# Splitting attention weights: low parts by an accumulating transfer, q and k normalised on VectorE

## Chip, cores and metric

One of the cores of a Trainium2 chip runs the whole program: five engines (TensorE, written PE in the profile, with its weight loads as PEld; VectorE, DVE; ScalarE, ACT; GpSimd, POOL; SyncE, SP, which here only issues transfers) and 16 DMA engines. The metric is the device time of one execution in microseconds. Lower is better.

## What is computed

A causal decoder trunk of two layers over 512 tokens of width 1024, in float32. Each layer is an attention block and a squared-ReLU MLP, both behind an RMSNorm:

```python
def reference(x, ...):
    for layer in range(DEPTH):                       # 2
        h = rms_norm(x, g_mix[layer])
        x = x + (even_mixer if layer % 2 == 0 else odd_mixer)(h, ...)
        h = rms_norm(x, g_mlp[layer])
        x = x + squared_relu_mlp(h, w_up[layer], w_down[layer])
    return x

def odd_mixer(h, w_in, b_forget, c_q_gain, c_k_gain, w_out):
    proj = jnp.einsum("bsd,de->bse", h, w_in)
    q = rms_norm(proj[..., :w].reshape(bsz, seq, 16, 64), c_q_gain)
    k = rms_norm(proj[..., w:2 * w].reshape(bsz, seq, 16, 64), c_k_gain)
    ...
    y = forgetting_attention(q, k, v, log_f)
    return jnp.einsum("bse,ed->bsd", y, w_out)
```

The even mixer does the same with two kinds of heads (eight with dilated windows, "a"; eight with a window of 128 and sinks, "b"), the odd one with sixteen forgetting heads ("c"). q and k are normalised per head.

## The kernel before

**Split products.** Every large product is made of three TensorE passes over numbers of the type fp32r. A weight W is split into a high part `whi` (W copied, and so rounded, to fp32r) and a low part `wlo` = W - `whi`; the activations are split likewise, and a product is x_hi·whi + x_hi·wlo + x_lo·whi (lines 230 to 232 in the projections, 163, 166 and 167 in `mm3` elsewhere).

**Weights of the attention.** `load_w` (line 177) fetches a tile `wraw` of 128 x 1024 numbers by SP and cuts it into parts of 128 x 512, which `parts` (line 169) hands to `split` (line 146). An entry of a pattern says who does what: the first word is the engine of `whi` (`act`: a ScalarE copy, line 149; `pool`: a GpSimd multiplication by 1.0, line 151), the second that of the subtraction for `wlo` (line 154, VectorE or GpSimd). `PAT_ATT` is for the projections, `PAT_OP` for the output projection, `PAT_START` (`act`, `dve`) for the first projections of each layer and for `kv_b`; a counter goes through a pattern part by part. There are four `wraw` buffers (the tiles `xl` of the residual use them too) and seven each of `whi` and `wlo`. With 8 parts for 512 columns, 4 for 256, 8 for the 272 of `vf_c` and 16 for an output projection, the two attention layers have 52 and 68 parts: 64 go by `PAT_ATT`, 32 by `PAT_OP`, 24 by `PAT_START`, of which 4 are those of `kv_b`. The MLP splits its weights elsewhere (`halves`, lines 768 and 769).

**Normalisation.** `norm_heads` (line 239) copies a projection's four token tiles out of PSUM, squares and sums them by head, takes reciprocal roots (`rsqrt_small`, lines 128 to 133) and multiplies (line 259). `NORM = 'vgvg'` gives the multiplications of tiles 0 and 2 to VectorE and of 1 and 3 to GpSimd. Eight calls make 32 multiplications, 28 of them 512 wide.

**Heads.** `prep_q` and `prep_k` transpose q and k by TensorE and split them (lines 276, 277, 158, 159); the halves of K are swapped by a transfer from SBUF to SBUF on SP (line 289). `scores` makes a head's scores, the maxima (VectorE, line 338), the exponentials (ScalarE, 341) and multiplies by the reciprocal sums: GpSimd does three of the four tiles (line 349), ScalarE one (346). `values` transposes these (361), splits them (373 and 374) and multiplies by v (381).

**Order.** `run` (line 429) interleaves the generators of the heads with those of the next projection or of the output projection, and `out_part` (line 461) is the dense work at the end of each attention; the MLP follows. Beyond that the library arranges each engine's instructions when the program is built, by its own estimates of when their inputs are ready; only what is marked `keep_in_program_order` keeps its place. On the chip each engine takes its instructions in that fixed order, and so does each engine's queue of transfers: a transfer that waits holds those behind it.

Of the kernel before, what the change touches and what calls it, by code (L numbers as in the profile page):

```python
# [9 lines left out]
F32 = mybir.dt.float32  # L10
# [3 lines left out]
AF = mybir.ActivationFunctionType  # L14
OP = mybir.AluOpType
# [14 lines left out]
RAW = 4  # L30
NHI = 7
NLO = 7
PAT_OP = (('pool', 'pool'), ('pool', 'dve'), ('pool', 'dve'), ('act', 'pool'))
SQ = (4, 4, 5, 5, 6, 6, 7, 7, 10)
R = 6
PAT_START = (('act', 'dve'), ('act', 'dve'))
WARM = 24
NORM = 'vgvg'
PSC = 'ggga'
GRAIN = 4  # L40
STARTPIN = 4
# [22 lines left out]
LAGS = (1, 1, 1)  # L64
NB = 86
PAT_MLP = (("act", "dve"),)
PAT_ATT = (('pool', 'dve'), ('pool', 'pool'))
YLO = 'dve'
SSQ = "vector"

# [1 line left out]
def trunk(ctx, tc, x, g_mix, g_mlp, w_in_even, a_q_gain, a_k_gain, b_q_gain, b_k_gain, b_sinks,  # L72
          w_out_even, w_in_odd, b_forget, c_q_gain, c_k_gain, w_out_odd, w_up, w_down, out):
    nc = tc.nc
# [4 lines left out]
    act = ctx.enter_context(tc.tile_pool(name="act", bufs=14))  # L79
# [4 lines left out]
    def bank(tag, name):  # L84
        return ps.tile([P, 512], F32, tag=tag, bufs=BANKS[tag], name=name)
# [56 lines left out]
    def in_order(m):  # L142
        if cnt["start"]:
            tc.keep_in_program_order(m)

    def split(dst_h, dst_l, src, eng, lo="dve"):

        if eng == "act":
            in_order(nc.scalar.copy(dst_h, src))  # L149
        elif eng == "pool":  # L150
            nc.gpsimd.tensor_scalar(dst_h, src, 1.0, 1.0, op0=OP.mult, op1=OP.mult)  # L151
        else:
            nc.vector.tensor_copy(dst_h, src)
        in_order((nc.gpsimd if lo == "pool" else nc.vector).tensor_sub(dst_l, src, dst_h.bitcast(F32)))  # L154
# [14 lines left out]
    def parts(src, eng):  # L169

        shape = list(src.shape)
        hi = wp.tile(shape, F32R, tag="whi", bufs=NHI, name="whi")
        lo = wp.tile(shape, F32R, tag="wlo", bufs=NLO, name="wlo")
        split(hi, lo, src, *eng)
        return hi, lo

    def load_w(srcs, w, kw, pat):
# [13 lines left out]
    def layer_attention(li, hT, w_in, w_out, stats=None):  # L191


        with ExitStack() as c2:
# [10 lines left out]

            def project(cols, use, pat=PAT_ATT, ahead=False):

                n = sum(b - a for a, b in cols)
                outs = [bank("pA", f"pj{t}") for t in range(NT)]
                pairs = 0  # L210
                kw = 4 if n == 256 else 2
                w = 1024 // kw if n <= 512 and n in (256, 512) else n
                for k0 in range(0, DC, kw):
                    srcs, o = [], 0
                    for a, b in cols:
                        srcs.append((0, o, w_in[k0 * P:(k0 + kw) * P, a:b]))
                        o += b - a
                    ws = load_w(srcs, w, kw, pat)
                    if ahead:
                        yield 0  # L220

                    last = k0 + kw == DC
                    for m in range(NT if last else kw):
                        for k, t in ([(k0 + kk, m) for kk in range(kw)] if last else [(k0 + m, t) for t in range(NT)]):
                            kk = k - k0
                            o = outs[t][:, :n]
                            ts = slice(t * P, (t + 1) * P)
                            xh, xl = hT[k][:, 0, ts], hT[k][:, 1, ts]
                            hi, lo = ws[kk]
                            nc.tensor.matmul(o, xh, hi[:, :n], start=k == 0, stop=False)  # L230
                            nc.tensor.matmul(o, xh, lo[:, :n], start=False, stop=False)  # L231
                            nc.tensor.matmul(o, xl, hi[:, :n], start=False, stop=k == DC - 1)  # L232
                            pairs += 1
                            if pairs % GRAIN == 0:
                                yield GRAIN / 32 * n
                use(outs)
                yield 0

            def norm_heads(outs, nh, sq_tag="sq", sq_bufs=1 + li):
# [16 lines left out]
                for t in range(NT):  # L256
                    q = qk[t // 2][:, t % 2, :w].rearrange("p (h d) -> p h d", d=HD)
                    eng = nc.gpsimd if NORM[t] == "g" else nc.vector
                    eng.tensor_mul(q, q, rs[:, t, :nh].unsqueeze(2).to_broadcast([P, nh, HD]))
# [188 lines left out]
            def out_weights(pairs, c0):  # L448
# [4 lines left out]
                while k < np_:  # L453
# [4 lines left out]
                    k = m + 1  # L458
                return load_w(runs, w, np_, PAT_OP)

# [47 lines left out]
            if li == 0:  # L508
                def qk_a(g):
                    return project([(g * 256, g * 256 + 256), (512 + g * 256, 512 + g * 256 + 256)], qk_use(g, 8),  # L510
                                   *((PAT_START, True) if g == 0 else ()))

                def v_a(g):
                    return project([(1024 + g * 256, 1024 + g * 256 + 256)], v_use(g, 0), PAT_START if g == 0 else PAT_ATT)

                def att_a(g):
                    def get(p_):
                        qk = st["qk", g]
                        return prep_q(qk, p_ * P), prep_k(qk, 256 + p_ * P, gg[:, 0:1])
                    return attend(get, 256, lambda: st["v", g], lambda j: j, "a", 4 * g, 2, 2 * g)  # L520

                def kv_b():
                    def use(outs):
                        st["v", 3] = prep_v(outs, P, 2, 1)
                        st["k", "b"] = norm_heads(outs, 2)
                    return project([(2048, 2304)], use, PAT_START)

                def att_b():
                    def get(p_):
                        if p_ == 0:  # L530
                            st["kb"] = prep_k(st["k", "b"], 0, gg[:, 1:2])
                        k = st["kb"][p_ // 2]
                        return prep_q(st["qk", "b"], p_ * P), [k, k]
                    return attend(get, 0, lambda: st["v", 3], lambda j: j // 4, "b", 0, 4, 4)

                tables, first, qk0 = make_tables(ap, dist, lt, lb), start(ap, hT), qk_a(0)
                next(tables)
                for i, n in enumerate((1, 1 + 8 // GRAIN, 1 + 8 // GRAIN, 1 + 8 // GRAIN)):
                    cnt["start"] = i < STARTPIN
                    next(first)  # L540
                    for _ in range(n):
                        next(qk0)
                    if i == 0:
                        next(tables)
                cnt["start"] = False
                for _ in range(8 // GRAIN):
                    next(qk0)
                next(first)
                all_of(qk0)
                all_of(v_a(0))  # L550
                run(att_a(0), 32, chain(kv_b(), project([(1536, 2048)], qk_use("b", 8))), 768, LEADS[0])
                run(att_b(), NB, chain(qk_a(1), v_a(1)), 768, LEADS[1])
                run(chain(att_a(1), last_values()), 38, chain(out_part([0, 1, 4, 5], True),
                                                              out_part([6, 7], False), ahead([2, 3])), 1536, LEADS[2])
                last = [2, 3]
            else:
                def qk_c(g):
                    return project([(g * 256, g * 256 + 256), (1024 + g * 256, 1024 + g * 256 + 256)], qk_use(g, 8))

                def v_c(g):  # L560
                    return project([(2048 + g * 256, 2048 + g * 256 + 256)], v_use(g, g))

                def vf_c():
                    def use(outs):
                        forget(ap, outs)
                        v_use(0, 0)(outs)
                    return project([(2048, 2304), (3072, 3088)], use, PAT_START)

                def att_c(g):
                    def get(p_):  # L570
                        qk = st["qk", g]
                        return prep_q(qk, p_ * P), prep_k(qk, 256 + p_ * P, gg[:, 2:3])
                    return attend(get, 256, lambda: st["v", g], lambda j: j, "c", 4 * g, 2, 2 * g)

                g = vf_c()
                for _ in range(STATS):
                    next(g)
                stats()
                all_of(g)
                all_of(qk_c(0))  # L580
                for g in range(3):
                    run(att_c(g), 36, chain(qk_c(g + 1), v_c(g + 1)), 768, LEADS[3 + g])
                run(chain(att_c(3), last_values()), 42, chain(out_part([0, 1, 2, 3], True),
                                                              out_part([4, 5], False), ahead([6, 7])), 1536, LEADS[6])
                last = [6, 7]
# [659 lines left out]
```

## Time and profile before

| | before |
|---|---|
| median of 3 runs | 1168.34 us (1167.92 to 1168.7) |
| profiled execution, its own time | 1168.43 us |
| its span | 1166.7 us |
| granted TensorE clock | 0.999 |
| attention of layer 0, about | 0 to 229 us |
| MLP of layer 0, about | 229 to 572 us |
| attention of layer 1, about | 572 to 829 us |
| MLP of layer 1, about | 829 us to the end |

The span is what the profile shows of one execution; 1.7 us of its time lie around it. The stages are read from the first instructions of each in the timeline; a stage's first weights are split before it begins. A busy TensorE isn't TensorE at its peak: matmuls overlap, each shown from its start to a modelled end.

### The profile page before, as it was taken

To read this page: it belongs to the slowest core of one execution; us is meant where nothing else is said; L and a number is where in the kernel's file an instruction comes from. 1 tells how busy PE (TensorE), PEld (TensorE's weight loads), DVE (VectorE), ACT (ScalarE), POOL (GpSimd) and SP (SyncE) were. 2 spreads that over 40 slices of the span, in tenths; PEclk is the share of its full clock that TensorE was granted. 3 is DMA by queue.
4 is the path that set the end of the run, shared out by engine and by line. 5 is a ranking of instruction groups with operands and counts; after the bars stand their busy time and mean duration, and the time that the engine had idled before them with its cause. 6 is when DMAs were issued, how large, how long until landed. Compare 5 with 4: busy or idle time off the path is not lost.

```text
span 1166.7 us, 17503 instructions
## 1 busy us (share of the span) xinstructions
PE 1146.8 (98%) x6256; PEld 982.5 (84%) x6256; DVE 880.7 (75%) x1877; ACT 647.1 (55%) x1349; POOL 202.4 (17%) x296
## 2 busy tenths in 40 slices
PE   8999989999999999999999999999999999999998
PEld 7987877888988988988887888888888888888887
DVE  7878999968858857855647877788858759669676
ACT  6555867556545545444235675656756455465452
POOL 1345444200000000000255445332100000000000
PEclk9999999999999999999999999999999999999999
DMA  7522014242333333333443333343430721623403
GB/s 253 163 76 89 19 57 146 70 126 78 104 108 91 91 108 91 106 111 110 146 128 109 107 84 109 107 118 113 163 105 4 235 87 55 198 73 109 147 33 109
DMA packets 100655, 126.57 MB, mean 108 GB/s; under 512 B 6184, under 2 KB 79944, under 8 KB 100568
## 3 DMA queue, kind: packets, MB, share of 16 engines
q1 hardware_dynamic: 99384, 121.23, 34.3%
q10 hardware_dynamic: 608, 2.13, 0.5%
q0 software_dynamic: 576, 2.10, 0.4%
q8 instruction: 49, 0.80, 0.3%
q14 instruction: 38, 0.31, 0.1%
HBM read 112.29 MB, written 6.32 MB: 102 GB/s over the span
## 4 chain that ended last, share of the span: by engine, by line
PE 85%; DVE 8%; DMA 2%; POOL 1%; issue 1%; ACT 1%; SPq 0%; ACTq 0%; POOLq 0%; DVEq 0%
PE up L163 10%; PE up L167 10%; PE up L166 10%; PE pj L230 5%; PE pj L232 5%; PE pj L231 5%; PE O L381 3%; PE PT L361 2%; PE Y L1021 2%; PE Y L1019 2%; PE Y L1022 2%; PE op L167 2%; PE op L163 2%; PE op L166 2%; PE Y L1068 1%; PE S L324 1%
## 5 line engine op out<-in xcount | busy, mean ns | idle before, releaser
L163 PE MATMUL up<-xin,whi 128*128 128x512 f32 x512 | 200.5, 392 | 0.0
L167 PE MATMUL up<-xin,whi 128*128 128x512 f32 x512 | 199.3, 389 | 0.0
L166 PE MATMUL up<-xin,wlo 128*128 128x512 f32 x512 | 199.2, 389 | 0.0
L768 ACT CAST whi<-wraw 128x512 fp32r<-128x512 f32 x228 | 139.2, 619 | 105.0 <-PE up L167 47.7
L769 DVE TENSOR_TENSOR wlo<-wraw,whi 128x512 fp32r<-128x512 f32 x228 | 151.7, 686 | 50.8 <-ACT whi L768 50.5
L167 PEld LDWEIGHTS up<-xin,whi 128*128 128x128 f32 x512 | 96.1, 188 | 20.1
L166 PEld LDWEIGHTS up<-xin,wlo 128*128 128x128 f32 x512 | 96.2, 188 | 19.8 <-issue 0.2
L163 PEld LDWEIGHTS up<-xin,whi 128*128 128x128 f32 x512 | 96.1, 188 | 19.8 <-issue 0.2
L341 ACT ACTIVATE P<-P,negm 128x128 f32<-128x128 f32 (+5 forms) x128 | 69.5, 544 | 51.7 <-DVE negm L338 47.9
L950 ACT ACTIVATE u<-up 128x512 f32<-128x512 f32 x64 | 38.3, 599 | 90.9 <-PE up L167 90.8
L230 PE MATMUL pj<-whi,hn 128*128 128x512 f32 (+2 forms) x256 | 88.7, 346 | 0.0
L232 PE MATMUL pj<-whi,hn 128*128 128x512 f32 (+2 forms) x256 | 86.9, 339 | 0.0
L231 PE MATMUL pj<-wlo,hn 128*128 128x512 f32 (+2 forms) x256 | 86.8, 339 | 0.0
L151 POOL TENSOR_SCALAR whi<-wraw 128x512 fp32r<-128x512 f32 x88 | 60.5, 689 | 143.0 <-PE pj L232 121.8
L789 DVE TENSOR_TENSOR t<-u 128x256 f32<-128x256 f32 x56 | 23.2, 424 | 62.8 <-ACT u L1093 61.0
L154 POOL TENSOR_TENSOR wlo<-wraw,whi 128x512 fp32r<-128x512 f32 x48 | 64.4, 1346 | 20.7 <-ACT whi L149 17.9
L230 PE MATMUL pj<-whi,h 128*128 128x512 f32 (+1 forms) x192 | 66.5, 353 | 0.7 <-DVE v L159 0.7
L232 PE MATMUL pj<-whi,h 128*128 128x512 f32 (+1 forms) x192 | 65.5, 343 | 0.0
L231 PE MATMUL pj<-wlo,h 128*128 128x512 f32 (+1 forms) x192 | 65.5, 341 | 0.0
L349 POOL TENSOR_SCALAR P<-P,rden 128x256 f32<-128x256 f32 (+2 forms) x96 | 47.7, 500 | 90.8 <-DVE rden L344 90.0
L154 DVE TENSOR_TENSOR wlo<-wraw,whi 128x512 fp32r<-128x512 f32 (+1 forms) x72 | 49.9, 700 | 17.7 <-POOL whi L151 14.5
L373 ACT CAST PT<-PT 128x256 fp32r<-128x256 f32 (+3 forms) x128 | 49.5, 405 | 19.4 <-PE PT L361 18.5
(229 smaller groups left out, 3054.4 us busy)
## 6 DMA issues: line engine op xcount, KB each, us to landing
wraw<-in_w_up SPq DMA_DIRECT2D x64, 512.0 KB, 3.8
wraw<-in_w_down SPq DMA_DIRECT2D x56, 512.0 KB, 4.2
wraw<-in_w_in_odd SPq DMA_DIRECT2D x36, 256.0 KB, 3.3
mraw<-in_w_down SPq DMA_DIRECT2D x16, 512.0 KB, 4.4
K<-K SPq DMA_DIRECT2D x26, 256.0 KB
wraw<-in_w_in_even SPq DMA_DIRECT2D x10, 512.0 KB, 4.0
wraw<-in_w_in_even SPq DMA_DIRECT2D x16, 256.0 KB, 4.5
xl<-xsp SPq DMA_DIRECT2D x8, 512.0 KB
```

The costliest lines, as they stand in the source:

```text
L151: nc.gpsimd.tensor_scalar(dst_h, src, 1.0, 1.0, op0=OP.mult, op1=OP.mult)
L154: in_order((nc.gpsimd if lo == "pool" else nc.vector).tensor_sub(dst_l, src, dst_h.bitcast(F32)))
L163: m = nc.tensor.matmul(o, wh, xh, start=start, stop=False, skip_group_check=more)
L166: nc.tensor.matmul(o, wl, xh, start=False, stop=False, skip_group_check=more)
L167: nc.tensor.matmul(o, wh, xl, start=False, stop=stop, skip_group_check=more)
L230: nc.tensor.matmul(o, xh, hi[:, :n], start=k == 0, stop=False)
L231: nc.tensor.matmul(o, xh, lo[:, :n], start=False, stop=False)
L232: nc.tensor.matmul(o, xl, hi[:, :n], start=False, stop=k == DC - 1)
L341: nc.scalar.activation(p[:, :ne], p[:, :ne], AF.Exp, scale=-1.0, bias=negm[:, i:i + 1], accum_out=den[:, i:i + 1])
L373: nc.scalar.copy(dst[:, 0], pt[:, :n])
L768: sca(nc.scalar.copy(dst_h, src))
L769: late.append(lambda: vec(nc.vector.tensor_sub(dst_l, src, dst_h.bitcast(F32))))
```

## The change

The 64 parts of `PAT_ATT`, the 32 of `PAT_OP` and the 4 of `kv_b`, which now takes `PAT_ATT`, get their low parts in another way. `lo` is first written with minus W, rounded to fp32r as `whi` is, by the one of GpSimd and ScalarE that does not make `whi`; then a transfer that GpSimd issues adds `wraw` onto it, which leaves W - `whi`. The two engines swap roles from part to part. No subtraction is left for these 100 parts; the 20 other parts of the attention are split as before. And all multiplications of `norm_heads` go to VectorE.

```diff
-PAT_OP = (('pool', 'pool'), ('pool', 'dve'), ('pool', 'dve'), ('act', 'pool'))
+PAT_OP = (('pool', 'dma'), ('act', 'dma'))
-NORM = 'vgvg'
+NORM = 'vvvv'
-PAT_ATT = (('pool', 'dve'), ('pool', 'pool'))
+PAT_ATT = (('pool', 'dma'), ('act', 'dma'))
...
         hi = wp.tile(shape, F32R, tag="whi", bufs=NHI, name="whi")
         lo = wp.tile(shape, F32R, tag="wlo", bufs=NLO, name="wlo")
-        split(hi, lo, src, *eng)
+        if eng[1] == "dma":
+
+            if eng[0] == "act":
+                nc.scalar.copy(hi, src)
+                nc.gpsimd.tensor_scalar(lo, src, -1.0, 1.0, op0=OP.mult, op1=OP.mult)
+            else:
+                nc.gpsimd.tensor_scalar(hi, src, 1.0, 1.0, op0=OP.mult, op1=OP.mult)
+                nc.scalar.activation(lo, src, AF.Copy, scale=-1.0)
+            nc.gpsimd.dma_start(lo.bitcast(F32), src, accum_op=OP.add)
+        else:
+            split(hi, lo, src, *eng)
         return hi, lo
...
-                    return project([(2048, 2304)], use, PAT_START)
+                    return project([(2048, 2304)], use)
```

## The prediction

> **What bounds the kernel now.** I read the page first, then the busy time of the engines by stretch, then what TensorE waited for in each stretch of the attention, then the chain of work through those waits.
>
> ```profile
> PE 1146.8 (98%) x6256; PEld 982.5 (84%) x6256; DVE 880.7 (75%) x1877; ACT 647.1 (55%) x1349; POOL 202.4 (17%) x296
> ```
>
> TensorE is busy for 98% of the span, and the change takes no matmul away; only the time in which TensorE waits can shrink. Where it lies:
>
> ```profile
> 25.00:225.00 200.00, 192.34 (x1145) 164.48 (x1144) 174.27 (x488) 129.78 (x336) 85.12 (x139) 1.00 0.32 96
> 225.00:575.00 350.00, 349.49 (x2025) 309.84 (x2024) 252.38 (x465) 180.85 (x327) 0.31 (x1) 1.00 0.34 103
> 600.00:825.00 225.00, 221.87 (x1327) 189.05 (x1326) 174.14 (x459) 136.34 (x322) 96.30 (x125) 1.00 0.38 108
> ```
>
> The columns are stretch, length, then busy time of PE, PEld, DVE, ACT, POOL, the granted clock, DMA share and GB/s. The middle row, an MLP, has TensorE idle for 0.5 us of 350. The two attention stretches have it idle for 200 - 192.3 = 7.7 and 225 - 221.9 = 3.1 us. That is a ceiling of about 11 us (0.9%) for anything done to the attention's other engines. A finer cut shows where VectorE is the cause:
>
> ```profile
> 125.00:150.00 25.00, 24.98 (x175) 21.93 (x174) 23.46 (x82) 22.08 (x67) 12.34 (x32) 1.00 0.08 23
> 150.00:175.00 25.00, 21.79 (x143) 19.13 (x141) 24.51 (x71) 15.18 (x42) 8.03 (x15) 1.00 0.22 66
> ```
>
> At 150 to 175 us VectorE is busy for 24.5 of 25 and TensorE for 21.8: there TensorE waits for VectorE. The waits of TensorE themselves, from the view of waits taken by stretch (the first two rows from 100 to 125 us, two from 150 to 175, one from 175 to 200, the last from 575 to 650; total, times, longest):
>
> ```profile
> PE qkT L266 <- DVE qk L259: 1.3, 2, 0.9
> PE S L324 <- DVE Q L277: 0.3, 1, 0.3
> ...
> PE S L324 <- DVE yf L385: 1.6, 1, 1.6
> PE S L324 <- DVE Q L277: 1.5, 1, 1.5
> ...
> PE PT L361 <- DVE negm L338: 0.8, 2, 0.6
> ...
> PE S L324 <- DMA K<-K: 2.1, 2, 1.1
> ```
>
> Together 1.6 + 3.1 + 0.8 + 2.1 = 7.6 us that end on VectorE or on a transfer that VectorE's work releases. This is what the change can win.
>
> **Part 1: work moved between engines.**
>
> ```profile
> L154 DVE TENSOR_TENSOR wlo<-wraw,whi 128x512 fp32r<-128x512 f32 (+1 forms) x72 | 49.9, 700 | 17.7 <-POOL whi L151 14.5
> L154 POOL TENSOR_TENSOR wlo<-wraw,whi 128x512 fp32r<-128x512 f32 x48 | 64.4, 1346 | 20.7 <-ACT whi L149 17.9
> L151 POOL TENSOR_SCALAR whi<-wraw 128x512 fp32r<-128x512 f32 x88 | 60.5, 689 | 143.0 <-PE pj L232 121.8
> L149 ACT CAST whi<-wraw 128x512 fp32r<-128x512 f32 x24 | 14.5, 627 | 4.0 <-DMA wraw<-in_w_out_odd 2.5 <-PE pj L232 1.2 <-PE op L167 0.2
> L259 POOL TENSOR_TENSOR qk<-qk,rs 128x512 f32<-128x512 f32 x14 | 18.9, 1367 | 15.1 <-DVE rs L133 14.6 <-issue 0.4
> L259 DVE TENSOR_TENSOR qk<-qk,rs 128x512 f32<-128x512 f32 x14 | 17.1, 1262 | 0.2
> L769 DVE TENSOR_TENSOR wlo<-wraw,whi 128x512 fp32r<-128x512 f32 x228 | 151.7, 686 | 50.8 <-ACT whi L768 50.5
> L641 POOL DMA_DIRECT2D xsp<-xs x4 | 2.4, 607 | 15.4 <-ACT xs L639 15.4
> ```
>
> Of 72 subtractions on VectorE 52 go (48 by the old patterns, 4 of kv_b): -52 x 0.70 = -36.4 us. The normalisation goes from 14 multiplications to 28. Before, two run on VectorE at 1262 ns while two run on GpSimd; the MLP's subtraction of the same width, with GpSimd idle, takes 686. Alone, 28 x 0.69 = 19.3 us against 17.1, +2.2. Sum for VectorE about -34 us of some 348 in the two stretches. GpSimd loses 48 x 1.35 + 14 x 1.37 = 84 us; it gets 100 - 88 = 12 copies more (8 us) and 100 issues, for which the nearest row is the plain one at 0.61 us (61 us). ScalarE does 100 copies instead of 12: +88 x 0.63 = +55 us, in stretches where it is idle for 70 and 89. That cover is thin only at 125 to 150 us, where it has 2.9 us left and four parts fall (2.5 us): cost between 0 and 2.5, I take 0.5, since the copies are early work that can slide.
>
> **Part 2: the waits on VectorE, one by one.** From VectorE's timeline, the fourth row from GpSimd's:
>
> ```profile
> 148.28 1.02 DVE L252 TENSOR_SCALAR ssv<-ss,ecol 128x8 f32<-128x8 f32 x1
> 149.29 1.52 DVE L307 SCALAR_TENSOR_TENSOR bias<-dist,lb 128x256 f32<-128x256 f16 x1
> 151.24 0.68 DVE L154 TENSOR_TENSOR wlo<-wraw,whi 128x512 fp32r<-128x512 f32 x1
> ...
> 147.98 2.54 POOL L154 TENSOR_TENSOR wlo<-wraw,whi 128x512 fp32r<-128x512 f32 x2
> ...
> 150.82 0.41 DVE L307 SCALAR_TENSOR_TENSOR bias<-dist,lb 128x256 f32<-128x256 f16 x1
> ```
>
> Ahead of the two waits at 151.5 and 161 us stands a subtraction of 0.7 us, and a bias step that takes 1.52 instead of 0.41 while GpSimd subtracts. VectorE is full from there to the second wait, so what is taken from it comes off the waits: 0.7 + 1.1, and some 0.4 of the slowed row at 148.28, are 2.2 of the 3.1 us. The normalisation inside (two multiplications before, four after) stays at about 2.7 us.
>
> At 104 us the wait for line 259 stays for the most part: four times 0.69 end 0.4 us later than two slow pairs, less one subtraction before them; 0.5 us of 1.6 goes. At 190 to 195 us, and ahead of the two waits for K, the chain of waits has
>
> ```profile
> 192.40 2.00 DVE wlo L154 x2
> ...
> 619.70 1.09 DVE wlo L154
> 622.30 3.25 DMA K<-K
> ...
> 641.92 0.69 DVE wlo L154
> ```
>
> two subtractions of 2.0 us, one of 1.09, one of 0.69. TensorE waits 0.8 us behind the first two and about 1.05 behind each of the others, so 0.8 + 1.1 + 0.7 go. Sum of gains: 2.2 + 0.5 + 0.8 + 1.8 = 5.3 us.
>
> **Part 3: the low part comes later.** Before, the last part of an attention takes 0.62 us for `whi` and 1.30 for `wlo` on GpSimd: 1.92 from the start of its first copy. After, both copies run side by side (0.62), then the issue (0.61), then the transfer. No accumulating transfer is in the trace. The nearest rows: SBUF to SBUF, 256 KB, as here, is K<-K above (64 partitions of 2 x 512 numbers) with 3.25 us; and the one GpSimd issues, 512 KB to DRAM:
>
> ```profile
> xsp<-xs POOLq DMA_DIRECT2D x4, 512.0 KB, 6.4
> ```
>
> An accumulating one reads two operands. I take 4.0 us, nearer to K<-K, which has its size and place. The low part is then ready after 0.62 + 0.61 + 4.0 = 5.2 us, 3.3 later than now (2.6 later at 3.25, 5.7 later at 6.4). Who covers this: the lead of each low part over its first matmul. The shortest in a projection that the change touches is that of layer 1's first part (the first two rows below: 585.82 - 577.99 = 7.8 us), enough for 5.7. At the end of each output projection it is shorter. GpSimd's last low parts there, and the matmuls that read them:
>
> ```profile
> 576.73 1.26 POOL L154 TENSOR_TENSOR wlo<-wraw,whi 128x512 fp32r<-128x512 f32 x1
> ...
> 585.82 0.48 PE L231 MATMUL pj<-wlo,hn 128*128 128x512 f32 x1
> ...
> 220.52 1.30 POOL L154 TENSOR_TENSOR wlo<-wraw,whi 128x512 fp32r<-128x512 f32 x1
> 819.65 2.56 POOL L154 TENSOR_TENSOR wlo<-wraw,whi 128x512 fp32r<-128x512 f32 x2
> ...
> 224.91 0.39 PE L166 MATMUL op<-y,wlo 128*128 128x512 f32 x1
> 824.95 0.39 PE L166 MATMUL op<-y,wlo 128*128 128x512 f32 x1
> ```
>
> At the ends the leads are 224.91 - 221.82 = 3.1 and 824.95 - 822.21 = 2.7 us, against 3.3 us: 0.2 + 0.6 = 0.8 us of new waits.
>
> The Trainium skill, page "DMA: Bandwidth & Descriptors", section "Anatomy of one DMA", gives 2.0 us plus the bytes over 436 GB/s for a transfer issued by GpSimd, which makes an estimate of 2.6 us for 256 KB. K<-K's 3.25 us is above it, so the row decides; by the page's figure the 0.8 us would be 0.
>
> **Part 4: the queues.** The transfer reads `wraw`, so a `wraw` buffer also comes free 3.3 us later, and SP's loads wait for just that; behind them in SP's queue stand K<-K, the biases and `xl`.
>
> ```profile
> SPq L182 <- DVE wlo L154: 110.4, 20, 27.4
> ...
> 642.64 0.37 SPq L182 DMA_DIRECT2D wraw<-in_w_in_odd  x1
> 644.33 4.52 SPq L289 DMA_DIRECT2D K<-K  x2
> ...
> POOL P L349 <- DVE rden L344: 90.0, 56, 9.3
> ```
>
> At 642.64 a load goes right as its buffer comes free, 1.3 us (after its own 0.37) ahead of a K<-K for which TensorE then waits. 3.3 us later, it would hold that K<-K by 2.0 us, unless the build puts it behind; I take half, 1.0. In GpSimd's queue 50 of the 100 issues wait for a ScalarE copy (the other 50 only for GpSimd's own), and behind them stand the multiplications of line 349. Those arrive 90.0/56 = 1.6 us early on the average, and the row of line 154 above has 17.9 us of waiting for ScalarE in it: bound 0 to 4 us, I take 0, since each head's values are read only beside the next head's scores.
>
> **The sum**, on the profiled execution's 1168.43 us (0.1 above the median, so for the median as well): -5.3 + 0.5 + 0.8 + 1.0 = -3.0, so 1165.4 us. Of this kernel about 0.2%, 2.3 us, can be told from no change.
>
> **Rivals.** *The transfer lands late (slower).* If it takes 6.4 us, as GpSimd's own transfer does, the low part comes 5.7 us later; the ends then pay 2.6 + 3.0, SP's queue (5.7 - 1.3)/2 = 2.2, ScalarE 0.5: 8.3 against 5.3, 1171.4 us. It decides from the lateness y at which the ends' 2y - 5.8, ScalarE's 0.5 and SP's (y - 1.3)/2 make 5.3: y = 4.5 us, a landing of 5.2 us. For it speaks the two-operand read, against it that xsp has twice the bytes and goes to DRAM. Chance 0.25. The Trainium skill, page "SBUF — State Buffer", section "SBUF: two separate sides", has a mechanism for it: while VectorE holds, in one of its two-port modes, the ports that it shares with GpSimd, GpSimd can't write the transfer's descriptors and the transfer waits. No run here shows it yet.
>
> *VectorE wasn't it (no change).* The waits for K and for the normalised q and k stay (1.8 + 0.5 of what I counted), because the new transfers share the DMA engines with K<-K and VectorE gets twice the multiplications: -5.3 + 2.3 + 2.3 = -0.7, 1167.7 us. For it: K<-K takes 3.3 us of each such chain, and nothing shortens it. Against it: the subtractions stand in the same chains. Chance 0.18.
>
> *All waits go.* 7.6 us less, with a landing like K<-K, the ends covered and 0.6 left of SP's price ((2.6 - 1.3)/2): 1161.4 us. For it: the slowed VectorE rows beside GpSimd's subtractions are more than I counted. Chance 0.12. The forecast has the remaining 0.45.
>
> **Numbers.** The range goes from 1160.8 (7.6 us of waits gone, nothing paid) to 1171.8 (the late landing, and a little of GpSimd's bound). The forecast's own range is 1162.5 to 1167.5. Faster by over 0.2%: 0.36 of the forecast's 0.45, 0.12 of the last rival, 0.02 of the second: 0.50. Within 0.2%: 0.07 of the forecast and the second's other 0.16: 0.23. Slower: the first rival and 0.02 of the forecast: 0.27.
>
> **What would show it.** VectorE's busy time falls by about 34 us, ScalarE's rises by 55, GpSimd's stays near 190. Line 259 runs at 0.69 us. The waits of TensorE at 151 and 161 us shrink to about 1 us, those for K<-K vanish. New waits for `wlo` by a transfer appear at the ends of the output projections, below 1 us each. Wrong would be: a transfer over 5.2 us from issue to landing; TensorE waiting for `wlo` in a projection; K<-K issued later because a load of `wraw` stands before it; line 349 delayed by an issue in front of it.

## The result, and the profile after

The changed kernel takes 1208.99 us (median, 1200.81 to 1213.87) against 1168.52 us for the kernel before on the same chip: a ratio of 1.0345, 95% interval 1.0304 to 1.0386. It is slower by 40 us where a gain of 3 was forecast, and far above the range, which ended at 1171.8. The profiled execution, the slowest of the four, took 1213.87 us, its span is 1212.1 and its mean granted clock 0.981 (0.999 before).

Lines of the changed kernel stand 10 further down than before from `load_w` on: the loads of `wraw` are line 192, K<-K is 299, the normalising multiplication 269, the scores' matmul 334. New are the copies 177 (`whi`) and 181 (-W) on ScalarE, 178 (-W) and 180 (`whi`) on GpSimd, and 182, the accumulating transfer. First the engines, from the page after:

```profile
PE 1164.1 (96%) x6256; PEld 994.2 (82%) x6256; DVE 845.0 (70%) x1841; ACT 695.5 (57%) x1437; POOL 209.3 (17%) x344
```

The same 6256 matmuls keep TensorE busy for 17.3 us longer (1164.1 against 1146.8), and TensorE is idle for 1212.1 - 1164.1 = 48.0 us against 19.9: +28.1. Together they are the 45.4 us by which the span grew. VectorE is relieved as forecast: 845.0 against 880.7.

Where: busy time by stretch, after (stretch, length, PE, PEld, DVE, ACT, POOL, granted clock, DMA share, GB/s).

```profile
25.00:225.00 200.00, 189.09 (x1116) 162.06 (x1115) 152.51 (x465) 142.32 (x361) 87.73 (x158) 0.98 0.60 142
225.00:575.00 350.00, 349.32 (x2012) 308.63 (x2012) 254.47 (x466) 181.78 (x329) 2.69 (x4) 1.00 0.34 103
600.00:825.00 225.00, 204.23 (x1181) 173.21 (x1180) 130.12 (x378) 139.52 (x320) 91.30 (x136) 0.95 0.66 152
600.00:625.00 25.00, 25.00 (x112) 20.71 (x111) 9.02 (x23) 9.92 (x18) 14.40 (x19) 1.00 1.01 225
```

and the last of these stretches before:

```profile
600.00:625.00 25.00, 24.62 (x113) 20.15 (x111) 15.57 (x30) 8.06 (x13) 13.78 (x15) 1.00 0.33 101
```

The MLP in the middle is as it was. In the attention of layer 1 TensorE is idle for 20.8 us of 225 (3.1 before), and the DMA engines' share has gone from 0.38 to 0.66; in the 25 us ahead of the first scores they are full (1.01, from 0.33). What TensorE waited for, after:

```profile
PE S L334 <- DMA K<-K: 29.8, 9, 5.6
PE S L334 <- ACT wlo L181: 3.0, 1, 3.0
PE op L166 <- DMA wlo<-wraw: 2.0, 2, 1.7
```

The waits for K<-K were 2.6 us in three before. They alone grew by 27.2 us, nearly as much as the whole idle time. One of them, by the chain of waits after (start, length, what):

```profile
623.49 6.49 DMA wlo<-wraw
...
630.17 0.37 SPq L192
630.59 0.46 SPq L192
631.10 5.97 DMA K<-K
637.21 0.55 PE S L334
```

and VectorE's timeline for the K that it moves:

```profile
627.40 0.74 DVE L159 SCALAR_TENSOR_TENSOR K<-qkT,gg,K 64x512 fp32r<-64x512 f32 x1
```

K is ready at 628.14. Its transfer stands in SP's queue behind two loads of weights, and these wait until the accumulating transfer that reads their raw buffer has landed, at 629.98. So K<-K is issued at 631.10, 2.96 us late, and then takes 5.97 us where the same step took 3.25 before, beside the loads just issued. Over all 26 K<-K the time from the end of the instruction that writes K to the issue sums to 16.7 us (1.2 before).

The longer busy time is the clock. Rows of the same view around these waits:

```profile
631.00:637.00 6.00, 0.57 (x3) 0.15 (x1) 0.00 (x0) 0.00 (x0) 1.50 (x2) 0.73 1.00 227
637.00:641.00 4.00, 3.79 (x15) 2.84 (x15) 1.46 (x9) 1.83 (x6) 0.55 (x2) 0.56 0.74 186
667.00:671.00 4.00, 4.00 (x19) 3.17 (x19) 2.24 (x8) 2.73 (x9) 0.85 (x2) 0.50 0.01 2
```

After a wait of 5.6 us TensorE works at a clock of about 0.5 for some microseconds. The trace has eight such windows at waits, of 3.4 or 6.8 us each, 41.0 us together; beside them it has one at the start, as before has. Half-rate work of up to 41.0 us costs up to 20.5, and 17.3 is what the busy time gained. The Trainium skill, page "TensorE: Matmul & The Clock Gate", section "Part 1: The HAM clock gate", says that a window of about 3.4 us without work drops TensorE to half rate, until a busy window of the same length has passed. This trace agrees on the half rate and on the length (3.4 and 2 x 3.4), but not on the time without work: four of the eight windows stand at waits of 1.7 to 3.0 us.

### The profile page after: what moved, and what is told of

It reads as the page before. It is cut to its first block, busy times and chain, and to the rows that moved or that the text cites. A ratio compares the mean times of both kernels' runs of the same rounds, so it can differ in the third digit from the quotient of the medians.

```text
span 1212.1 us, 17819 instructions
## 1 busy us (share of the span) xinstructions
PE 1164.1 (96%) x6256; PEld 994.2 (82%) x6256; DVE 845.0 (70%) x1841; ACT 695.5 (57%) x1437; POOL 209.3 (17%) x344
## 4 chain that ended last, share of the span: by engine, by line
PE 83%; DMA 8%; DVE 4%; ACT 2%; issue 2%; POOL 1%; SPq 0%; POOLq 0%; DVEq 0%; ACTq 0%
PE up L163 10%; PE up L167 10%; PE up L166 10%; PE pj L240 4%; PE pj L242 4%; PE pj L241 4%; DMA K<-K 4%; PE PT L371 3%; DMA wlo<-wraw 3%; PE O L391 3%; PE S L334 2%; PE Y L1032 2%; PE Y L1031 2%; PE Y L1029 2%; PE op L167 2%; PE S L335 2%
## 5 line engine op out<-in xcount | busy, mean ns | idle before, releaser
L182 POOL DMA_DIRECT2D wlo<-wraw x100 | 91.4, 928 | 26.0 <-POOL wlo L178 12.3
L348 DVE CUSTOM_DVE_ANT_0 P<-S,bias 128x128 f32<-128x128 f32 (+1 forms) x96 | 46.0, 486 | 61.7 <-PE S L337 49.6
L334 PE MATMUL S<-K,Q 128*128 128x256 f32 (+2 forms) x128 | 51.0, 402 | 32.8 <-DMA K<-K 29.8
L371 PE MATMUL PT<-ident,P 128*128 128x128 f32 x296 | 58.4, 298 | 2.2 <-DVE PT L384 1.2
```

The source lines that it names most:

```text
L182: nc.gpsimd.dma_start(lo.bitcast(F32), src, accum_op=OP.add)
L334: nc.tensor.matmul(s[:, :n], qs, k[:, 0, k0:k0 + n], start=True, stop=False)
L371: nc.tensor.transpose(pt[:, (i - c) * P:(i - c + 1) * P], pr[i][:, kb * P:(kb + 1) * P], ident)
```

## The experiments

Three theories. **Q**, the queue: a raw buffer is held until the transfer has landed, so SP's loads, and K<-K behind them, go late. **S**, the share: the transfers' traffic takes the 16 DMA engines from K<-K and the loads. **N**: the normalisation on VectorE alone. Times are medians, with the ratio to the kernel before on the same chip (1167.5 to 1167.9).

**N: one half of the change at a time.** The transfers with the old normalisation (`NORM = 'vgvg'` in the kernel after), and the new normalisation alone (`NORM = 'vvvv'` in the kernel before).

> The changed kernel with the normalisation shared by VectorE and GpSimd again (vgvg). Theories Q and S: the loss stays, 1203 to 1214 us. Theory N: back to about 1170.

> The kernel before with vvvv alone: all multiplications of the normalisation on VectorE. Theories Q and S: between 1165 and 1171, no measurable part of the loss. Theory N, already weakened by the run of the transfer alone (1209.7): 1180 or more.

Measured: 1209.66 us (1.0363, 1.0343 to 1.0384) and 1173.22 us (1.0050, 1.0035 to 1.0065). The transfers make all of the loss. The normalisation alone costs 5.4 us, more than Q and S had left it and less than N had: with VectorE still subtracting it adds 5.0 us of VectorE's time (885.7 us busy), and a wait of 2.5 us behind VectorE appears at 161 us with a half-rate window after it. Beside the transfers it costs nothing measurable.

**Where: only the projections' parts by transfer.**

```diff
-PAT_OP = (('pool', 'dma'), ('act', 'dma'))
+PAT_OP = (('pool', 'pool'), ('pool', 'dve'), ('pool', 'dve'), ('act', 'pool'))
```

> The changed kernel with the old pattern for the output projections, so that only the 68 parts of the projections use the transfer. Theory Q and S alike: nearly all waits for K<-K in layer 1 up to 760 us stay, those at the ends for wlo go: 1197 to 1205. If the ends (the prediction's place) carried the loss, it would be below 1180.

Measured: 1194.44 us (1.0226, 1.0209 to 1.0244); K<-K issued late by 15.0 us in sum. The 68 parts of the projections cost 27 us (with the new normalisation, which this run keeps), the 32 of the output projections the other 14.5, beyond the 4 to 12 that the expectation left them.

**Q: K<-K past the loads.** K<-K is issued by ScalarE, so that it stands behind no load; with the same edit of the kernel before as a control.

```diff
-                    nc.sync.dma_start(k[r2].bitcast(F32), k[r].bitcast(F32))
+                    nc.scalar.dma_start(k[r2].bitcast(F32), k[r].bitcast(F32))
```

> The changed kernel with one line moved: the swap of K's halves (K<-K) is issued by ScalarE, no longer by SP. Theory Q (the queue: a wraw buffer comes free only when its accumulating transfer has landed, so SP's loads of wraw wait for that and stand, waiting or freshly released, ahead of K<-K): TensorE's waits for K<-K fall from 29.8 us to under 6 and the time from 1209 to about 1178. Theory S (the share: 25 MB more on the same 16 DMA engines slow every K<-K, whoever issues it): the waits stay over 20 us and the time over 1200. Theory N (normalising on VectorE alone is what costs): no change, about 1209.

> Control: the kernel before with the same line moved. All theories expect little, since there SP issues every K<-K within 0.1 us of K being ready: 1165 to 1172 us. If it gains more than 4 us, that much of the run with K<-K on ScalarE is not the change's.

Measured: 1185.17 us (1.0164, 1.0126 to 1.0202), control 1174.31 (1.0078, 1.0049 to 1.0108), above what was expected of it. The new queue costs 6.8 us by itself and still takes 23.8 us off. The waits, of the kernel after with this edit:

```profile
PE S L334 <- DMA K<-K: 11.6, 8, 4.5
```

11.6 us in place of 29.8: the queue is a large part of the cause, and not all.

**Q: the raw buffer let go.** The transfer adds `whi`, so that nothing but the two copies reads `wraw`; sizes, issues and places stay. The low parts are left out by that: -W and `whi`, rounded alike, add up to about nothing (and not to a low part of the wrong sign, as the expectations have it).

```diff
-            nc.gpsimd.dma_start(lo.bitcast(F32), src, accum_op=OP.add)
+            nc.gpsimd.dma_start(lo.bitcast(F32), hi.bitcast(F32), accum_op=OP.add)
```

> The changed kernel, but the accumulating transfer adds whi instead of wraw, which leaves the low parts with the wrong sign. Transfers, copies and queues stay as many and as large; only wraw is free as soon as the two copies have read it. Theory Q: SP's waits for the transfers are gone, TensorE's waits for K<-K fall under 8 us, time about 1176. Theory S: the traffic is the same, so over 1200. Theory N: about 1209.

> Both queue remedies at once: K<-K issued by ScalarE, and the transfer adds whi instead of wraw (low parts with the wrong sign). Theory Q (both of the earlier remedies take away parts of one queue effect): 1174 to 1178, little over the control with K<-K on ScalarE, 1174. Theory S (what each remedy left is the traffic of the accumulating transfers): it stays above 1183, since the traffic is whole.

Measured: 1192.97 us (1.0216, 1.0177 to 1.0256), and with K<-K on ScalarE's queue as well 1191.13 (1.0206, 1.0190 to 1.0222). Without the hold K<-K is issued on time (late by 1.3 us in sum), 16.0 us are gone, and the other queue adds nothing. 25 us of loss are left with no late issue. Q alone falls. What is left, in the kernel that adds `whi`: the stretch ahead of the first scores of layer 1, and K<-K in the chain of waits.

```profile
600.00:625.00 25.00, 25.00 (x116) 20.79 (x115) 11.35 (x26) 11.89 (x21) 13.20 (x18) 1.00 0.99 223
```

```profile
624.38 5.41 DMA K<-K
```

The DMA engines are still full there, and K<-K, on time, takes 5.41 us.

**S: fewer bytes.** As the kernel that adds `whi`, but the transfer moves 128 of the 512 columns of a part, then 256 (the rest of each low part stays -W).

```diff
-            nc.gpsimd.dma_start(lo.bitcast(F32), src, accum_op=OP.add)
+            nc.gpsimd.dma_start(lo[:, 0, :256].bitcast(F32), hi[:, 0, :256].bitcast(F32), accum_op=OP.add)
```

> The kernel whose transfer adds whi, with the transfer cut to the first 128 of 512 columns; the rest of the low part keeps minus W. Count of transfers, issues, copies and order of dependences as in the run that adds whi (1193 us), bytes a quarter. Theory S: TensorE's waits for K<-K fall from 15 to under 6 us, time 1176 to 1181. Theory Q and any theory of the number of issues or of the copies: stays near 1190.

> The kernel after with the accumulating transfer cut to 256 of the 512 columns of each part (128 KB) and adding the high part's columns, as the quarter did; half of each low part stays the negated weights, so part of the computation is left out. Theory S (bytes of the accumulating transfers take the DMA engines from the K<-K transfers) with a price in proportion to the bytes: a third of the way from 1168.9 (64 KB) to 1193.0 (256 KB), so 1174 to 1180 us, with waits of TensorE for K<-K near 7 us. S with a threshold (the engines have room until their share in the stretches of loading comes near 1.0): 1168 to 1172, the waits at 3 to 5 us. If the issue or the copies cost something, the quarter would have shown it.

Measured: 1168.87 us for the quarter (1.0007, 0.9997 to 1.0018), 1174.70 for the half (1.0057, 1.0041 to 1.0072), against 1192.97 for the whole. Issues and copies are the same in all three, so the 24.1 us go with the bytes. The landing of the low part goes with them too, and with it the time for which `whi` is held, which these runs don't part from the traffic. The first quarter costs nothing measurable, net of VectorE's relief; the second costs 5.8, the other two 9.1 each; the interval of the whole is some 4.6 us either way, so 5.8 and 9.1 needn't differ. The kernel with the quarter (its lines of the heads stand 4 further down), by stretch:

```profile
25.00:225.00 200.00, 194.93 (x1148) 166.23 (x1147) 158.73 (x475) 147.09 (x369) 90.92 (x161) 0.99 0.44 109
600.00:625.00 25.00, 25.00 (x119) 20.73 (x118) 13.00 (x32) 13.21 (x24) 13.05 (x18) 1.00 0.61 132
```

TensorE's waits for K and for the low parts, with the quarter, the half and the whole:

```profile
PE S L338 <- DMA K<-K: 3.7, 3, 2.5
PE op L166 <- DMA wlo<-whi: 1.5, 1, 1.5
...
PE S L334 <- DMA K<-K: 6.1, 5, 3.3
PE op L166 <- DMA wlo<-whi: 3.1, 2, 2.5
...
PE S L334 <- DMA K<-K: 15.3, 9, 3.8
PE op L166 <- DMA wlo<-whi: 4.4, 3, 2.9
```

With the quarter the DMA share ahead of the scores is 0.61, and the waits for K<-K are nearly back to 2.6. From the quarter to the whole they grow by 11.6 us and those for a late low part by 2.9, so the late landing carries the smaller share of what the profile shows as waits.

**The hold at a quarter of the bytes.** The quarter-size transfer reads `src[:, 0, :128]` again, as the change does.

> The kernel after with the transfer cut to 128 of the 512 columns, but adding the raw weights as the change does: the raw buffer is again held until the transfer has landed (three quarters of each low part stay the negated weights). Theory Q (the raw buffers come free late, so SP's loads of weights stand ahead of K<-K and push it) in its strong form: the raw buffers are held to the landing, which is only some 1 us earlier at 64 KB than at 256 KB, so 1185 to 1205 us, K<-K issued late by 10 us or more in sum. Theory S (bytes; a late raw buffer matters only because the landing is slowed by the same bytes): 1168 to 1174 us, K<-K issued late by under 6 us in sum.

Measured: 1175.19 us (1.0060, 1.0039 to 1.0081). It lies between the two expectations: K<-K is late by 4.2 us in sum and TensorE waits 10.5 us for it. The hold is worth 6.3 us here and 16.0 with whole transfers, so the causes may raise each other: the landing, until which a buffer is held, took 2.7 us here and 4.4 with whole transfers.

**Bytes without accumulation.** The kernel before, complete; after each split in the attention GpSimd also sends the high part to DRAM, where nobody reads it (120 such transfers, since the parts of `PAT_START` have one too); then 128 of its columns; then 128 columns of the raw weights.

```diff
         split(hi, lo, src, *eng)
+        dump = dram.tile(shape, F32, tag="dump", bufs=8, name="dump")
+        nc.gpsimd.dma_start(dump, hi.bitcast(F32))
```

> The kernel before, complete, and after each split of a weight part in the attention layers GpSimd also issues a plain transfer of the high part (256 KB, nothing accumulated) into DRAM that nobody reads: 100 transfers of the same size at the same places. Theory S (any bytes of that amount at that place do it, through the 16 DMA engines): slower, 1176 to 1195 us, waits for K<-K of 8 us or more. If instead the accumulation or the late low part itself is what costs: 1167 to 1173 us, waits for K<-K under 5 us.

> The kernel before, complete, with the same extra GpSimd transfers of high parts into DRAM as the run that took 1181.0 us, but 128 of the 512 columns of each (64 KB in place of 256): the issues are the same, only the bytes fall. If the bytes made the 13 us (theory S): 1168 to 1172 us. If GpSimd's time for issuing them (some 70 us of its time, in front of its subtractions and its multiplications of the heads' values) made them: 1177 to 1183 us.

> The kernel before, complete, with the 64 KB plain transfer into DRAM behind each part (1173.0 us), reading the raw weights in place of the high part: the same issues and the same bytes, but a raw buffer is held until that transfer has landed (2.2 us of landing, and GpSimd's time until the issue). Theory Q: K<-K is issued late again and the time rises by 5 to 15 us, to 1178 to 1188 us. Theory S, with 64 KB harmless: 1172 to 1175 us.

Measured: 1181.05 us (1.0118, 1.0099 to 1.0137), 1173.04 (1.0042, 1.0027 to 1.0057) and 1185.41 (1.0147, 1.0130 to 1.0164). Of the 13.3 us of the first, 8.0 go with the bytes and 5.3 stay with the issues and the small transfers. Plain bytes do harm too, but its waits for K<-K were 4.9 us, not the 8 expected: the loss lies in many places. The third costs 12.4 us more than the second, in the range that Q gave it, but not by the way that Q named: K<-K is late by 1.2 us in sum. A part of its chain of waits, what SP's loads waited for its small transfers, and GpSimd's timeline:

```profile
606.77 4.67 DMA wraw<-in_w_in_odd
...
611.96 0.49 POOL dump L176
...
614.91 3.78 DMA wraw<-in_w_in_odd
...
619.22 0.49 POOL dump L176
```

```profile
SPq L184 <- DMA dump<-wraw: 6.3, 5, 1.9
```

```profile
611.96 1.13 POOL L176 DMA_DIRECT2D dump<-wraw  x2 [2.80 <-DMA wraw<-in_w_in_odd]
613.12 1.21 POOL L151 TENSOR_SCALAR whi<-wraw 128x512 fp32r<-128x512 f32 x2
```

The loads of weights waited for a landing in five cases only, 6.3 us in sum (195.7 us in the kernel after). But the small transfers now need nothing but the load, and GpSimd issues two of them, 1.13 us, as soon as a load has landed, ahead of the copies to `whi`; the subtractions, the next load into the same buffer and so q and k come later by that. So this run changes GpSimd's order as well as the hold and can't price the hold.

**A small dose of the change, complete.** Every fourth part (24 of 96) by a whole accumulating transfer in place of a subtraction on VectorE, all else as before; then the same, adding `whi` (which leaves those 24 low parts out).

```diff
-PAT_OP = (('pool', 'dma'), ('act', 'dma'))
-NORM = 'vvvv'
-PAT_ATT = (('pool', 'dma'), ('act', 'dma'))
+PAT_OP = (('pool', 'pool'), ('pool', 'dve'), ('act', 'dma'), ('act', 'pool'))
+NORM = 'vgvg'
+PAT_ATT = (('pool', 'dve'), ('pool', 'pool'), ('act', 'dma'), ('pool', 'pool'))
-                    return project([(2048, 2304)], use)
+                    return project([(2048, 2304)], use, PAT_START)
```

> The complete computation: only every fourth part of the attention's projections and output projections (24 of 96) gets its low part by a whole accumulating transfer of 256 KB, each in place of a subtraction on VectorE; the others and the normalisation stay as before. Theory S by bytes: as much traffic as in the quarter-size run, so next to no loss, and VectorE is relieved of 24 x 0.70 = 17 us: 1165.5 to 1169 us. If a single transfer of the full size does its harm wherever it meets a K<-K or a raw buffer (its landing of 4.4 us, and not the sum of bytes): a quarter of the loss, 1174 to 1180 us. A time below 1165.4 would mean that the prediction's gain was there to be had.

> The kernel with every fourth part by a whole accumulating transfer (1184.5 us), the transfer adding the high part in place of the raw weights, so that the raw buffer comes free when the two copies are done (the low parts of those 24 parts come out wrong). Theory Q (a raw buffer held until GpSimd has got to the issue and the transfer has landed, and SP's queue behind the load that waits for it): nearly all of the 16.6 us goes, 1166 to 1172 us, K<-K issued late by under 3 us in sum. Theory S (the traffic itself): 24 transfers still move the same bytes, so 1180 to 1186 us.

Measured: 1184.51 us (1.0136, 1.0120 to 1.0153) and 1171.69 (1.0038, 1.0023 to 1.0053). The first is beyond both expectations: S by bytes alone falls, and the harm is not a quarter of the whole either. The hold is 12.8 of its 16.6 us. The DMA share at 600 to 625 us is 0.49, and the landing only 3.4 us. TensorE's waits for K<-K in the two, first with the hold:

```profile
PE S L334 <- DMA K<-K: 14.2, 7, 4.3
...
PE S L334 <- DMA K<-K: 5.3, 6, 1.9
```

K<-K is issued late by 12.0 us in sum with the hold and by 2.1 without. Ahead of the first scores SP's queue in the first has

```profile
603.75 25.13 SPq L192 DMA_DIRECT2D wraw<-in_w_in_odd  x8
628.93 1.11 SPq L299 DMA_DIRECT2D K<-K  x2
```

with K ready at 625.58, 3.35 us before the issue. Few transfers are enough if a load that waits for one stands ahead of K<-K. Here the transfer itself was issued late: GpSimd, which works in order, had two multiplications of the normalisation and the split of another part ahead of the issue.

**Does the relieved VectorE help at all?** The quarter-size transfers of `whi` with `NORM = 'vgvg'`.

> The kernel with the quarter-size transfer (128 columns, adding the high part; three quarters of each low part stay the negated weights) and q and k normalised by VectorE and GpSimd in turn, as before. Whether the relief of VectorE is worth what the prediction gave it: the norm on VectorE alone cost 5.4 us on the kernel before. If it costs the same where the low parts are off VectorE: 1162 to 1165 us. If the relieved VectorE takes the norm at no cost, as the pair of whole transfers said: 1168 to 1170 us, and then the relief buys nothing measurable by itself.

Measured: 1169.66 us (1.0015, 1.0005 to 1.0025). VectorE is relieved of 37 us (843.6 busy) with little traffic and no hold, and the time is no better than before. No kernel of the study beats the kernel before by more than its measurement can tell.

**The account.** On the way from before to after through these runs (about 1167.8): 1.1 us for the copies, issues and small transfers net of what VectorE's relief gives; 24.1 for the rest of the bytes; 16.0 for the hold: 41.2 together. Another way would divide it otherwise, since the hold and the bytes may raise each other.

## Why the prediction was wrong, point by point

**What bounds the kernel** was read rightly: TensorE, with 11 us of idle time in the attention that other engines could give back. No run gained anything that would test the ceiling. Nothing in the reading asked how much the waits could grow.

**Part 1** held. VectorE lost 35.7 us (forecast 34), ScalarE gained 48.4 (55), and the multiplications run at the forecast pace:

```profile
L269 DVE TENSOR_TENSOR qk<-qk,rs 128x512 f32<-128x512 f32 x28 | 18.7, 728 | 0.2
L182 POOL DMA_DIRECT2D wlo<-wraw x100 | 91.4, 928 | 26.0 <-POOL wlo L178 12.3
```

Mainly the issue was mis-sized: 928 ns against the plain one's 607, so that GpSimd is at 209 us and not at 190.

**Part 2** held for VectorE's part and failed for K. The waits at 151 and 161 us (3.1 us) are 1.2 in the kernel with the quarter, and TensorE's idle time at 25 to 225 us falls there from 7.7 to 5.1: 2.6 of the 3.5 us forecast for that layer. But the time didn't follow: that kernel's span keeps 1.2 us less idle time and 3.7 us more busy time, by two half-rate windows behind waits of about 2 and 2.5 us. Removed waits and their price at full clock were counted; what a new wait of 2 us costs beyond itself was not. The waits for K<-K, "vanish" in the forecast, grew to 29.8 us.

**Part 3** was near in the middle and not in the spread. The landing, from the page after and from the view of line 182:

```profile
wlo<-wraw POOLq DMA_DIRECT2D x100, 256.0 KB, 4.4
...
DMA to landing us min/median/max: 3.3/4.4/8.0
```

The median is 4.4 us against 4.0, but 36 of the 100 took over 5.2 us. TensorE's waits at the ends were 2.0 us against 0.8, and there were none for `wlo` in a projection. The estimate of 2.6 us by the Trainium skill, page "DMA: Bandwidth & Descriptors", section "Anatomy of one DMA", is far below the 4.4; the plain transfers to DRAM of 256 and 64 KB landed in 2.9 and 2.2 us, near its 2.6 and 2.15, so it holds here for these and not for the accumulating ones inside SBUF. The rival of a late landing had the sign, but not the place: it was to decide at 5.2 us, and to pay at the ends.

**Part 4 is the step that failed.** It said "I take half, 1.0": it looked for a load that goes right as its buffer comes free and stands ahead of a K<-K in the trace before, found one, at 642.64, and priced that one. The hold cost 16.0 us with whole transfers and 12.8 with a quarter of them. The priced K<-K was 0.15 us late in the end (it goes at 659.09 after). The place of the longest wait, 5.6 us, was in the trace before as well. SP's queue ahead of the first scores of layer 1, and VectorE's subtraction for which the loads wait there:

```profile
620.81 0.88 SPq L182 DMA_DIRECT2D wraw<-in_w_in_odd  x2
622.30 2.01 SPq L289 DMA_DIRECT2D K<-K  x2
...
619.70 1.09 DVE L154 TENSOR_TENSOR wlo<-wraw,whi 128x512 fp32r<-128x512 f32 x1 [3.47 <-POOL whi L151]
```

The two loads go as soon as the subtraction has freed their buffer, and are through at 621.69, 0.6 us ahead of a K<-K for which TensorE then waits. By the prediction's own rule a release 3.3 us later holds this K<-K by 2.7 us; after, the order here is the same and K<-K goes 2.96 us late. The rule was right here, but the prediction applied it to one of several such places, another one, and halved the price; a load at 666.49 ahead of a K<-K at 667.32 is a third. Nor is 3.3 us the lateness everywhere, since the landing took up to 8.0 us. In sum K<-K went 16.7 us late, and a half-rate window came on top at the longer waits.

**The term that was not there** is the traffic. The rows of Part 1 gave 100 x 256 KB = 26 MB, and the middle columns showed the DMA share, but the sum had no line for it. The second rival named the shared DMA engines and let the waits for K stay; they grew to 29.8 us. Bytes cost 24.1 us. Both causes pass through the clock: of the 45.4 us by which the profiled span grew, 17.3 are longer busy time, which fits the half-rate windows.

Of the signs listed, "K<-K issued later because a load of `wraw` stands before it" came, and so did "a transfer over 5.2 us from issue to landing", for 36 of the 100. The first rival's mechanism of shared ports wasn't tried.

## What to carry to other kernels

When work moves from an engine to a transfer, write its bytes and its holds into the sum like any busy time: how full the DMA engines are in the stretch where it falls, and which buffer now comes free only when it lands. Follow a late release to every urgent transfer that stands behind a load of these buffers, not only to one of them. And price a wait of the matrix engine of 2 us or more with the half-rate window that may follow it.

## What the runs showed of the hardware

**The accumulating transfers took the DMA engines about twice as long as plain ones to DRAM.** GpSimd's queue in the kernel after, and in the one with plain transfers to DRAM (packets, MB, share of 16 engines), with the issues and the landings of the latter:

```profile
q0 software_dynamic: 14976, 28.32, 13.1%
```

```profile
q0 software_dynamic: 9920, 32.58, 7.6%
...
L176 POOL DMA_DIRECT2D dump<-whi x120 | 69.9, 582 | 381.8 <-ACT whi L149 364.1
...
dump<-whi POOLq DMA_DIRECT2D x112, 256.0 KB, 2.9
```

Less the 2.10 MB and 0.4% that this queue has in the kernel before: 154 us of all 16 engines for 26.2 MB, so 1.54 us for 256 KB, against 85 us for 30.5 MB, so 0.73. No run has a plain transfer by GpSimd from SBUF to SBUF, so the accumulation isn't parted from the place that is written. The issue takes 928 ns against 582. The accumulating one landed after 4.4 us when it added the raw weights and after 5.6 when it added `whi`; why is open.

**Waits of 2 to 3 us already cost clock.** Over the 18 profiles, without the first 20 us of each, pauses between the starts of TensorE's matmuls beyond the usual spacing were followed by a half-rate window in 23 of 24 cases from 3 us up, in 17 of 39 from 2 to 3 us, and in 2 of 28 from 1.5 to 2. One from the kernel with the quarter, around a wait of 2.5 us for K<-K:

```profile
664.00:669.00 5.00, 2.48 (x13) 1.81 (x12) 0.00 (x0) 0.81 (x2) 0.88 (x1) 0.99 0.99 191
669.00:672.00 3.00, 3.00 (x15) 2.60 (x15) 1.48 (x8) 1.61 (x6) 0.36 (x1) 0.50 0.02 4
```

The Trainium skill, page "TensorE: Matmul & The Clock Gate", section "HAM oscillation — how this bites in real kernels", asks for no gaps over about 3.4 us; by these counts shorter gaps, from about 2 us, already cost clock in this kernel.
